# Chunks of the activation parts without padding, at constant places, in a two-block transformer kernel on Trainium2

## The chip, the cores and the metric

The kernel runs on one core of one Trainium2 chip. The metric is device time in microseconds (us) of one execution. Besides the times there is one profiled execution, whose trace gives every instruction's start and duration, engine by engine: PE is TensorE (matrix products), DVE VectorE, ACT ScalarE, POOL GpSimd, and SP the engine that issues nearly all DMAs. The operands of the matrix products lie in SBUF, a memory of 128 partitions; every place below is a byte address within a partition, and it is the same in all of them.

## The reference

Two transformer blocks follow each other on one sequence of 256 tokens with 1,024 features, all in float32.

```python
# first block
xn = rms_norm(x, g); proj = xn @ w_in                 # 1024 -> 3088
y  = concat(moba_attention(q, k, v), gated_linear_attention(...) * silu(gr))
x  = x + y @ w_out
h  = causal_dwconv(rms_norm(x) @ w_ffn_up)            # 1024 -> 2 * 2816
x  = rms_norm(x + (silu(h_gate) * h_val) @ w_ffn_down)
# second block
proj = rms_norm(x) @ w_in_2                           # 1024 -> 6916
ys = short_conv, spatial_gating, stick_breaking, forgetting attention
x  = x + (sum_n sigmoid(gate_n) * (ys_n @ w_branch_n)) @ w_out_2
g, u = split(rms_norm(x) @ w_ffn_in); out = x + (silu(g) * u) @ w_ffn_out
```

Nearly all of the arithmetic is products of 256 tokens with weight matrices that are read once.

## The kernel before

**Split products.** A float32 product is made from three matmuls in the float32r type (`mm3`, lines 184 to 187). Each operand is split into a high and a low part: high times high, low activations times high weights, high activations times low weights. In a matmul one operand is loaded into the array first (the weights, instruction LDWEIGHTS, shown as PEld) and the other streams past it (the moving operand).

**Weights.** The class `Stream` brings the weights in pieces of 128 x 2048 numbers (`raw`, three buffers). ACT copies one half of a piece, 1,024 numbers a partition, to `hi` (line 154) and DVE subtracts to get `lo` (line 155), in five buffers each. A half holds eight weight tiles of 128 numbers, 512 bytes a partition. A buffer of `hi` or `lo` is 4,096 bytes, so every weight tile begins at the same place modulo 512. Call that place 0 from here on: all places below are counted from it, modulo 512.

**Activations.** The moving operands are pairs of tiles (`xh`, `xl`), (`yh`, `yl`) with 8 chunks of 256 tokens (`KD` = 8), and (`hh`, `hl`) with 22 chunks (`KF` = 22). A chunk is 1,024 bytes a partition. In the kernel before the chunks are padded: `new_x` and `new_y` (lines 297 to 301) make tiles of `T + 8` columns and use the first `T`, so that a chunk begins 1,056 bytes behind the one before it, and its place moves by 32. `hh` and `hl` have `T + 4` columns (line 762), 1,040 bytes, and their place moves by 16 with each chunk. By the sizes of the tiles that lie between them, the high parts `xh` and `yh` begin at place 0 and the low parts `xl` and `yl` at 256; `hh` begins at 416 and `hl` at 256.

One pair is not made in these places: the merged branches of the second block, `mh` and `ml` (in `second`, tags `u8a` and `u8b`), have no padding. In the kernel as built all their chunks stand at place 192, before and after the change. Their matmuls are the second block's output projection, 64 weight tiles.

**Which pair feeds what.** In the order of the program, with the number of weight tiles (three matmuls each) whose moving operand the pair is:

- first `xh`, `xl`: normed input, 128 tiles of the first block's projections;
- first `yh`, `yl`: attention outputs, 64 tiles of `w_out`;
- second `xh`, `xl`: 96 tiles, the first six steps of the first feed-forward (`HELD` = 6);
- second `yh`, `yl`: 256 tiles, its other sixteen steps;
- first `hh`, `hl`: 176 tiles of its down projection;
- third `yh`, `yl`: 384 tiles of the second block's projections and gates;
- third `xh`, `xl`: 64 tiles of its branches;
- fourth `yh`, `yl`: 96 tiles of the second feed-forward;
- fourth `xh`, `xl`: its other 256 tiles;
- second `hh`, `hl`: 176 tiles of its down projection.

In `tm` the roles are the other way round: the activations are loaded into the array (half a chunk, 128 tokens) and 256 columns of weights stream, in 336 matmuls in all (lines 185 to 187 with `hi` or `lo` as the moving operand).

**What sets the order.** The program is recorded in the order of the code, and a scheduler orders each engine's instructions. The weights' splitting runs ahead of the matmuls by up to four halves (`AHEAD`). The attention parts are generators that `pump` advances between groups of matmuls. SP issues the loads in the order in which they are recorded: the first weights and `X`, then `late_loads` (lines 91 to 95), then the rest of the weights. `lv` holds masks that the gated linear attention reads on DVE (line 548).

Of the kernel before, what the change touches and what calls it, by code (L numbers as in the profile page):

```python
# [10 lines left out]
F32R = mybir.dt.float32r  # L11
BF = mybir.dt.bfloat16
I32 = mybir.dt.int32
# [5 lines left out]
D, T, FF = 1024, 256, 2816  # L19
KD, KF = D // 128, FF // 128  # L20
# [7 lines left out]
LEVELS = (1, 2, 4, 8, 16, 32)  # L28
# [24 lines left out]
def block_kernel(ctx: ExitStack, tc: tile.TileContext, xT, wst, sm_d, cs_d, lv_d, gup_d, out, dbg=None):  # L53
    nc = tc.nc
# [3 lines left out]
    def pool(name, bufs, **kw):  # L58
        return tc.tile_pool(name=name, bufs=bufs, reuse_waits="tile", **kw)

    const = ctx.enter_context(tc.tile_pool(name="const", bufs=1))
# [6 lines left out]
    def mm_tile():  # L68
        return mmp.tile([128, 512], F32, name="mm", tag="mm")

    def at_tile():
        return atp.tile([128, 512], F32, name="at", tag="at")
# [5 lines left out]
    X = resid.tile([128, KD, T], F32, name="X")  # L78
    sm = const.tile([128, SM_W], F32, name="sm")
    cs = const.tile([128, CS_W], F32, name="cs")  # L80
    lv = const.tile([128, len(LEVELS), 64], I32, name="lv")
    gup = const.tile([17, 256], F32, name="gup")
    nc.scalar.dma_start(out=sm[:, :SM_FIRST], in_=sm_d[:, :SM_FIRST])

# [6 lines left out]
    def late_loads():  # L91
        nc.sync.dma_start(out=cs, in_=cs_d)
        nc.sync.dma_start(out=sm[:, SM_FIRST:], in_=sm_d[:, SM_FIRST:])
        nc.sync.dma_start(out=lv, in_=lv_d)
        nc.sync.dma_start(out=gup, in_=gup_d)

    def par(name):
# [74 lines left out]
    st = Stream()  # L172
    st.load_to(3)
    late_loads()
    identb = const.tile([128, 128], BF, name="identb")
    V.tensor_copy(identb, ident)
# [12 lines left out]
    def fm(ps, xh, xl, ks, start=True, stop=True, steps=0, **kw):  # L189
        ks = list(ks)  # L190
        for n, k in enumerate(ks):
            wh, wl = st.tiles()
            mm3(ps, wh, wl, xh[:, k, :], xl[:, k, :], start and n == 0, stop and n == len(ks) - 1, **kw)
            if n % 4 == 3:
                pump(steps)

    def fm_pair(ps, xh, xl, between=None):

        for n, (a, k) in enumerate([(a, k) for a in range(2) for k in range(KD - 1)] + [(0, KD - 1), (1, KD - 1)]):
            wh, wl = st.tiles()  # L200
            mm3(ps[:, a * T:(a + 1) * T], wh, wl, xh[:, k, :], xl[:, k, :], n == 0, k == KD - 1,
                skip_group_check=True)
            if between and n == KD:
                between()
# [11 lines left out]
    def split_from(h, l, src):  # L216
        S.copy(h, src)
        V.tensor_tensor(l, src, f32(h), op=ALU.subtract)
# [75 lines left out]

    bigs = ctx.enter_context(tc.tile_pool(name="bigs", bufs=1))

    def new_x():
        return tuple(bigs.tile([128, KD, T + 8], F32R, name=n, tag=n)[:, :, :T] for n in ("xh", "xl"))

    def new_y():  # L300
        return tuple(bigs.tile([128, KD, T + 8], F32R, name=n, tag=n)[:, :, :T] for n in ("yh", "yl"))

    nwk = ctx.enter_context(tc.tile_pool(name="nwk", bufs=1))

# [72 lines left out]
    class Boundary:  # L377


        def __init__(self, g, sums=None, first=None, then=None):  # L380
            self.g, self.then = g, then or new_x
            self.h, self.l = (first or new_y)()
            self.ss = SumSq(nwk, "a")
            self.s2, self.g2 = (SumSq(nwk, "b"), sums) if sums is not None else (None, None)
# [18 lines left out]
        def finish(self):  # L403
            if self.s2 is None:
                v, t = (nwk.tile([128, T], F32, name="sq", tag="sq", bufs=3) for _ in range(2))
                self.rb = nwk.tile([128, T], F32, name="rb", tag="rb", bufs=2)
                V.tensor_scalar(v, self.p1, 1.0 / D, EPS, op0=ALU.mult, op1=ALU.add)
                newton(v, self.rb, t, True)
                return
            else:  # L410
                tc.keep_in_program_order(S.preload_act_table_set("natural_log_exp_and_others"))

                v = nwk.tile([128, 4], F32, name="v4")
                V.tensor_scalar(v[:, 0:2], self.p1, 1.0 / D, EPS, op0=ALU.mult, op1=ALU.add)
                V.tensor_scalar(v[:, 2:4], v[:, 0:2], EPS, None, op0=ALU.mult)
                V.scalar_tensor_tensor(v[:, 2:4], self.p2, 1.0 / D, v[:, 2:4], op0=ALU.mult, op1=ALU.add)
                r = inv_sqrt(v, 4, nwk)
                self.r1, r = r[:, 0:2], r[:, 2:4]
            self.r = r
            self.rb = spread(r, nwk)  # L420
# [6 lines left out]


    with pool("first", 1) as wk:
        ss = SumSq(nwk, "a")  # L430
        xh, xl = new_x()
        for k in range(KD):
            scaled(k, par("g_attn"), xh, xl)
# [16 lines left out]
        V.scalar_tensor_tensor(gq, pss[0].rearrange("p (a t) -> p a t", a=2), 0.125, rbb, op0=ALU.mult, op1=ALU.mult)  # L450
        V.tensor_tensor(gk, pss[1].rearrange("p (a t) -> p a t", a=2), rbb, op=ALU.mult)
        yh, yl = new_y()
        cosr = wk.tile([128, T], F32, name="cosr")
        sinr = wk.tile([128, T], F32, name="sinr")
# [281 lines left out]
        if "ya" in dbg:  # L736
            drain(t_gla)
            for k in range(KD):
                t = wk.tile([128, T], F32, name="dbgt")
# [5 lines left out]
        for half in range(2):  # L745
            for d in range(KD):
                a = accs[d // 2]
                fm(a[:, (d % 2) * T:(d % 2 + 1) * T], yh, yl, range(4 * half, 4 * half + 4),
                   start=(half == 0 and d % 2 == 0), stop=(half == 1), steps=2, skip_group_check=True)
                if half and d % 2:  # L750
                    if d == 1:
                        nb_ = Boundary(par("g_ffn"), first=new_x, then=new_y)
                    for e in (d - 1, d):
                        nb_.add(e, a[:, (e % 2) * T:(e % 2 + 1) * T])
            drain(t_gla)
# [3 lines left out]
    def gated_ffn(nb, emit, finish):  # L759

        with pool("ffn", 1) as wk:
            hh, hl = (wk.tile([128, KF, T + 4], F32R, name=n)[:, :, :T] for n in ("hh", "hl"))
            held = []

            def hidden(ps, j):
                split_from(hh[:, j, :], hl[:, j, :], emit(ps, j, wk))

            for j in range(KF):
                ps = mm_tile()
                if j == 0:  # L770
                    fm_pair(ps, nb.h, nb.l, nb.sums)
                    nb.finish()
                    nb.normed()
                else:
                    x = (nb.h, nb.l) if j < HELD else (nb.xh, nb.xl)
                    for half in range(2):
                        fm(ps[:, half * T:(half + 1) * T], *x, range(KD))
                if j < HELD:
                    t = wk.tile([128, 2, T], F32, name="held", tag="held", bufs=3)
                    V.tensor_tensor(t, ps.rearrange("p (a t) -> p a t", a=2),  # L780
                                    nb.rb[:, None, :].to_broadcast([128, 2, T]), op=ALU.mult)
                    hidden(t.rearrange("p a t -> p (a t)"), j)
                else:
                    hidden(ps, j)
            for d in range(KD):
                ps = mm_tile()
                fm(ps[:, :T], hh, hl, range(KF))
                finish(d, ps[:, :T], wk)
# [24 lines left out]
    def first_end(d, ps, wk):  # L813
        if not holder:
            holder.append(Boundary(ggm, par("g_fin")))
        holder[0].add(d, ps)

    gated_ffn(nb_, conv_emit, first_end)
    nb_ = holder[0]

    with pool("second", 1) as wk:
        yh, yl = new_x()
        fr = [wk.tile([128, 2, T], F32, name="fr", tag="t2", bufs=4) for _ in range(2)]
        pss = []
# [11 lines left out]
        xh, xl, rb, r = nb_.h, nb_.l, nb_.rb, nb_.r  # L839
# [22 lines left out]
        pl = at_tile()  # L862
# [31 lines left out]
        for hd in range(2):  # L894
            p, m = 64 - 64 * hd, 96 - 64 * hd
# [214 lines left out]
        if "yb" in dbg:  # L1110
            for k in range(KD):
                t = wk.tile([128, T], F32, name="dbgt")
# [28 lines left out]
    def second_end(d, ps, wk):  # L1141
        V.tensor_tensor(X[:, d, :], X[:, d, :], ps, op=ALU.add)
        nc.sync.dma_start(out=out[:, d, :], in_=X[:, d, :])

    gated_ffn(nb_, swiglu_emit, second_end)
    assert st.used == 16 * N_PIECES, st.used

# [158 lines left out]
```

## Time and profile before

| | |
|---|---|
| median of 3 runs | 751.35 us (750.97 to 751.64) |
| the profiled execution, its own time | 751.71 us |
| span of its trace | 750.0 us |
| PE busy | 736.9 us, 98% of the span |
| DVE, ACT, POOL busy | 71%, 56%, 15% of the span |
| granted TensorE clock, mean | 0.995 of full speed |

The profiled execution is 1.71 us longer than its span, and 0.36 us longer than the median. A matmul's duration in the trace (about 0.28 us) is its passage through the array; several are in it at a time. What counts for the time is the distance from one matmul's start to the next one's start, which the timeline gives to 0.01 us.

### The profile page before, as it was taken

To read this page: it belongs to the slowest core of one execution; us is meant where nothing else is said; L and a number is where in the kernel's file an instruction comes from. 1 tells how busy PE (TensorE), PEld (TensorE's weight loads), DVE (VectorE), ACT (ScalarE), POOL (GpSimd) and SP (SyncE) were. 2 spreads that over 40 slices of the span, in tenths; PEclk is the share of its full clock that TensorE was granted. 3 is DMA by queue.
4 is the path that set the end of the run, shared out by engine and by line. 5 is a ranking of instruction groups with operands and counts; after the bars stand their busy time and mean duration, and the time that the engine had idled before them with its cause. 6 is when DMAs were issued, how large, how long until landed. Compare 5 with 4: busy or idle time off the path is not lost.

```text
span 750.0 us, 14591 instructions
## 1 busy us (share of the span) xinstructions
PE 736.9 (98%) x6042; PEld 718.9 (96%) x6042; DVE 535.8 (71%) x805; ACT 423.2 (56%) x689; POOL 113.9 (15%) x125
## 2 busy tenths in 40 slices
PE   8997999999999999999999999999999999999998
PEld 7996889999999999999998999999999999999998
DVE  6679756899998776556785787766889855555441
ACT  7574666577767655545457476444467644444330
POOL 3067100214222111221000001100223100000000
PEclk9998999999999999999999999999999999999999
DMA  8742332364555554544443444554446555455530
GB/s 304 291 146 86 113 113 83 143 225 149 189 209 185 189 205 169 176 163 169 169 169 113 169 147 141 198 190 170 169 170 225 177 204 183 173 195 197 188 127 22
DMA packets 19813, 127.51 MB, mean 170 GB/s; under 512 B 2322, under 2 KB 3747, under 8 KB 5027
## 3 DMA queue, kind: packets, MB, share of 16 engines
q1 hardware_dynamic: 19602, 126.56, 47.7%
q8 instruction: 47, 0.77, 0.4%
q14 instruction: 20, 0.16, 0.1%
q10 hardware_dynamic: 144, 0.02, 0.0%
HBM read 125.52 MB, written 1.05 MB: 169 GB/s over the span
## 4 chain that ended last, share of the span: by engine, by line
PE 90%; DVE 6%; ACT 1%; DMA 1%; issue 1%; SPq 0%; DVEq 0%; ACTq 0%
PE mm L185 28%; PE mm L186 28%; PE mm L187 28%; DVE lo L155 2%; DMA X<-in_x 1%; PE at L698 1%; PE at L371 1%; DVE Qb L533 1%; DVE AT L548 1%; PE at L363 1%; DVE xl L283 0%; PE at L927 0%; PE at L372 0%; DVE cv L803 0%; PE at L942 0%
## 5 line engine op out<-in xcount | busy, mean ns | idle before, releaser
L155 DVE TENSOR_TENSOR lo<-raw,hi 128x1024 fp32r<-128x1024 f32 (+1 forms) x236 | 296.2, 1259 | 137.0 <-ACT hi L154 136.1
L154 ACT CAST hi<-raw 128x1024 fp32r<-128x1024 f32 (+1 forms) x236 | 244.5, 1041 | 216.7 <-PE mm L186 170.1
L185 PE MATMUL mm<-yh,hi 128*128 128x256 f32 x800 | 225.0, 283 | 0.8 <-DVE cv L803 0.8
L186 PE MATMUL mm<-yl,hi 128*128 128x256 f32 x800 | 224.0, 281 | 0.0
L187 PE MATMUL mm<-yh,lo 128*128 128x256 f32 x800 | 223.9, 281 | 0.0
L185 PE MATMUL mm<-xh,hi 128*128 128x256 f32 x544 | 153.8, 284 | 1.5 <-ACT hi L154 1.3
L187 PE MATMUL mm<-xh,lo 128*128 128x256 f32 x544 | 153.8, 285 | 1.1 <-DVE lo L155 1.0
L186 PE MATMUL mm<-xl,hi 128*128 128x256 f32 x544 | 152.6, 282 | 0.1
L185 PEld LDWEIGHTS mm<-yh,hi 128*128 128x128 f32 x800 | 150.1, 188 | 1.6 <-ACT hi L154 0.9
L186 PEld LDWEIGHTS mm<-yl,hi 128*128 128x128 f32 x800 | 150.8, 189 | 0.7 <-issue 0.6
L187 PEld LDWEIGHTS mm<-yh,lo 128*128 128x128 f32 x800 | 150.7, 188 | 0.1
L185 PEld LDWEIGHTS mm<-xh,hi 128*128 128x128 f32 x544 | 102.5, 189 | 2.9 <-ACT hi L154 2.1
L187 PEld LDWEIGHTS mm<-xh,lo 128*128 128x128 f32 x544 | 102.5, 189 | 2.8 <-DVE lo L155 2.1
L186 PEld LDWEIGHTS mm<-xl,hi 128*128 128x128 f32 x544 | 102.7, 189 | 0.7 <-DVE xl L283 0.5
L186 PE MATMUL mm<-hl,hi 128*128 128x256 f32 x352 | 99.0, 281 | 0.0
L187 PE MATMUL mm<-hh,lo 128*128 128x256 f32 x352 | 98.8, 281 | 0.0
L185 PE MATMUL mm<-hh,hi 128*128 128x256 f32 x352 | 98.5, 281 | 0.0
L186 PEld LDWEIGHTS mm<-hl,hi 128*128 128x128 f32 x352 | 66.4, 189 | 0.0
L187 PEld LDWEIGHTS mm<-hh,lo 128*128 128x128 f32 x352 | 66.3, 188 | 0.0
L185 PEld LDWEIGHTS mm<-hh,hi 128*128 128x128 f32 x352 | 66.1, 188 | 0.0
L277 POOL TENSOR_TENSOR ssa<-ssa,sq 128x256 f32<-128x256 f32 x20 | 18.7, 936 | 120.9 <-ACT sq L276 120.4
L806 POOL TENSOR_TENSOR cv<-cv 128x256 f32<-128x256 f32 x22 | 23.5, 1067 | 81.0 <-DVE cv L803 76.0
(333 smaller groups left out, 961.3 us busy)
## 6 DMA issues: line engine op xcount, KB each, us to landing
raw<-in_w SPq DMA_DIRECT2D x115, 1024.0 KB, 4.8
raw<-in_w SPq DMA_DIRECT2D x3, 512.0 KB, 8.3
out<-X SPq DMA_DIRECT2D x8, 128.0 KB, 1.9
sm<-in_sm SPq DMA_DIRECT2D x1, 814.5 KB, 13.4
X<-in_x SPq DMA_DIRECT2D x3, 256.0 KB, 7.3
cs<-in_cs SPq DMA_DIRECT2D x1, 706.0 KB, 11.3
raw<-in_w SPq DMA_DIRECT2D x2, 256.0 KB, 4.1
X<-in_x SPq DMA_DIRECT2D x2, 128.0 KB, 3.4
```

The costliest lines, as they stand in the source:

```text
L154: a = S.copy(hi[:, c:c + step], raw[:, c:c + step])
L155: b = V.tensor_tensor(lo[:, c:c + step], raw[:, c:c + step], f32(hi[:, c:c + step]), op=ALU.subtract)
L185: PE.matmul(ps, lh, rh, start=start, stop=False, **kw)
L186: PE.matmul(ps, lh, rl, start=False, stop=False, **kw)
L187: PE.matmul(ps, ll, rh, start=False, stop=stop, **kw)
L277: (V if self.n >= 6 else G).tensor_tensor(self.s, self.s, q, op=ALU.add)
L363: PE.transpose(pts[hd][:, j * 128:(j + 1) * 128], Ps[hd][:, j * 128:(j + 1) * 128], ident)
L371: PE.matmul(o, vs_[hd][0], PTs[hd][:, 0:256], start=True, stop=False, skip_group_check=True)
L533: V.tensor_tensor(q.rearrange("p x (n h) -> p x n h", h=h), qv[rows, :, :, 1, :], ev[rows, :, :, 1, :], op=ALU.mult)
L548: V.copy_predicated(o, lv[:, n, None, :].to_broadcast([128, 8, 64]).rearrange("p e (n h) -> p e n h", h=h), pm.rearrange("p (e n h) -> p e ...
L698: PE.matmul(ps[:, c:c + n], qb[:, a, hd, i * 128:(i + 1) * 128], kT[:, a, :n], start=True, stop=False, skip_group_check=True)
L806: G.tensor_tensor(c[0], c[0], c[1], op=ALU.mult)
```

## The change

`bigs` and the feed-forward pools no longer hold padded tiles. A new function `placed` makes a tile of `n * T + 128` columns and cuts out of it `n` chunks of `T` columns without padding, from column `first` on. All chunks of a part then stand at one place modulo 512. A list, `places`, names the first column for each pair in the order in which the pairs are made; both parts of a pair have the same one.

`X` and the new tiles of 8,704 bytes are multiples of 512, so `xh`, `xl`, `yh` and `yl` all begin at place 0, and a first column of 48 puts their chunks at place 192. `hh` and `hl` (23,040 bytes) both begin at 416, and column 72 puts them at 192. So the places are, in the order of the list above: 192, 208, 176, 192, 192, 192, 192, 160, 448 and 448. In `tm`, where the activations are loaded, the streaming weights stand at 320 against them throughout; before, that distance moved with the chunk.

To make room, `lv` leaves the pool `const` for the pool `first`, whose space later stages use again, and its load is recorded behind that of `gup`. Everything behind it in SBUF moves by 1,536 bytes, three times 512.

```diff
-    lv = const.tile([128, len(LEVELS), 64], I32, name="lv")
...
-        nc.sync.dma_start(out=lv, in_=lv_d)
         nc.sync.dma_start(out=gup, in_=gup_d)
...
+    places = {"x": [(48, 48), (44, 44), (48, 48), (112, 112)], "y": [(52, 52), (48, 48), (48, 48), (40, 40)],
+              "h": [(72, 72), (8, 8)]}
+
+    def placed(pl, name, n, first):
+
+        t = pl.tile([128, n * T + 128], F32R, name=name, tag=name)
+        return t[:, first:first + n * T].rearrange("p (k t) -> p k t", t=T)
+
+    def new_pair(c):
+        return tuple(placed(bigs, c + p, KD, o) for p, o in zip("hl", places[c].pop(0)))
+
     def new_x():
-        return tuple(bigs.tile([128, KD, T + 8], F32R, name=n, tag=n)[:, :, :T] for n in ("xh", "xl"))
+        return new_pair("x")
 
     def new_y():
-        return tuple(bigs.tile([128, KD, T + 8], F32R, name=n, tag=n)[:, :, :T] for n in ("yh", "yl"))
+        return new_pair("y")
...
     with pool("first", 1) as wk:
+        lv = wk.tile([128, len(LEVELS), 64], I32, name="lv")
+        nc.sync.dma_start(out=lv, in_=lv_d)
...
-            hh, hl = (wk.tile([128, KF, T + 4], F32R, name=n)[:, :, :T] for n in ("hh", "hl"))
+            hh, hl = (placed(wk, "h" + p, KF, o) for p, o in zip("hl", places["h"].pop(0)))
```

On PE, DVE and ACT the instructions stand in the same order before and after; only their addresses differ. On SP, early in the program, two loads change places. Before:

```order
L92 DMA cs<-in_cs 128x1412
L93 DMA sm<-in_sm 128x1629
L94 DMA lv<-in_lv 128x384
L95 DMA gup<-in_gup 17x256
L141 DMA raw<-in_w 128x2048 x109
```

After the change, at the same place of SP's order:

```order
L91 DMA cs<-in_cs 128x1412
L92 DMA sm<-in_sm 128x1629
L93 DMA gup<-in_gup 17x256
L441 DMA lv<-in_lv 128x384
L139 DMA raw<-in_w 128x2048 x109
```

The masks `lv` are now loaded behind the small table `gup`; the weights behind both keep their place.

## Rows read from the trace of the kernel before

**Rows 1.** The page: the span, each engine's busy time, the granted clock by slices.

```profile
span 750.0 us, 14591 instructions
PE 736.9 (98%) x6042; PEld 718.9 (96%) x6042; DVE 535.8 (71%) x805; ACT 423.2 (56%) x689; POOL 113.9 (15%) x125
...
PEclk9998999999999999999999999999999999999999
```

**Rows 2.** The page's chain of work that ended last, by engine.

```profile
PE 90%; DVE 6%; ACT 1%; DMA 1%; issue 1%; SPq 0%; DVEq 0%; ACTq 0%
```

**Rows 3.** PE's waits: line, waited for, us in total, times, longest us.

```profile
PE at L542 <- DVE Qb L533: 4.5, 2, 3.1
PE mm L185 <- ACT hi L154: 1.3, 1, 1.3
PE at L117 <- DVE ones L111: 1.1, 1, 1.1
PE mm L187 <- DVE lo L155: 1.0, 1, 1.0
PE mm L185 <- DVE cv L803: 0.8, 1, 0.8
PE at L698 <- DVE AT L548: 0.6, 1, 0.6
```

**Rows 4.** Timeline: start us, duration us, engine, line; a matmul and the weight loads.

```profile
708.70 0.28 PE L185 MATMUL mm<-hh,hi 128*128 128x256 f32 x1
708.70 0.19 PEld L186 LDWEIGHTS mm<-hl,hi 128*128 128x128 f32 x1
708.82 0.28 PE L186 MATMUL mm<-hl,hi 128*128 128x256 f32 x1
708.83 0.19 PEld L187 LDWEIGHTS mm<-hh,lo 128*128 128x128 f32 x1
...
709.07 0.28 PE L185 MATMUL mm<-hh,hi 128*128 128x256 f32 x1
```

**Rows 5.** Timeline, PE: chunk nine of the same output, and chunk ten's start.

```profile
710.49 0.28 PE L185 MATMUL mm<-hh,hi 128*128 128x256 f32 x1
...
710.83 0.28 PE L185 MATMUL mm<-hh,hi 128*128 128x256 f32 x1
```

**Rows 6.** Timeline, PE: first matmul of the output projection, and of what follows.

```profile
535.86 0.28 PE L185 MATMUL mm<-mh,hi 128*128 128x256 f32 x1
...
558.47 0.28 PE L185 MATMUL mm<-yh,hi 128*128 128x256 f32 x1
```

**Rows 7.** Timeline, PE: second feed-forward, fourth x pair's first, hh's first and last matmul.

```profile
592.93 0.28 PE L185 MATMUL mm<-xh,hi 128*128 128x256 f32 x1
...
683.81 0.28 PE L185 MATMUL mm<-hh,hi 128*128 128x256 f32 x1
...
746.29 0.28 PE L187 MATMUL mm<-hh,lo 128*128 128x256 f32 x1
```

**Rows 8.** Timeline, PE: first feed-forward, matmul behind a wait, hh's first, the next stage.

```profile
203.75 0.28 PE L186 MATMUL mm<-yl,hi 128*128 128x256 f32 x1
...
271.78 0.28 PE L185 MATMUL mm<-hh,hi 128*128 128x256 f32 x1
...
334.39 0.28 PE L185 MATMUL mm<-yh,hi 128*128 128x256 f32 x1
```

**Rows 9.** Timeline, PE: the first block's output projection, first matmul, and of what follows.

```profile
121.65 0.28 PE L185 MATMUL mm<-yh,hi 128*128 128x256 f32 x1
...
144.28 0.28 PE L185 MATMUL mm<-xh,hi 128*128 128x256 f32 x1
```

**Rows 10.** Timeline, PE: chunk six of the fourth x pair, and chunk seven's start.

```profile
595.07 0.28 PE L185 MATMUL mm<-xh,hi 128*128 128x256 f32 x1
...
595.42 0.28 PE L185 MATMUL mm<-xh,hi 128*128 128x256 f32 x1
```

**Rows 11.** The tile lv: its DMA and its reads, and its time to landing.

```profile
L548 DVE COPY_PREDICATED AT<-lv,at x6: 686/718/1321, 58.9 to 83.0; 128x512 f32<-128x512 int32 x6
L94 SPq DMA_DIRECT2D lv<-in_lv x1: 328/328/328, 10.0 to 10.0; - x1
...
DMA to landing us min/median/max: 12.6/12.6/12.6
```

## The prediction

> **What bounds the kernel now.** I read the page's busy times first. PE is busy for 98% of the span, and the granted clock reads nine tenths or more of the upper level, 2.4 GHz, in 39 of 40 slices [rows 1], so nothing is to be had there. The chain of waits says the same: 90% of what set the end is PE, 6% DVE [rows 2]. The waits that ended idle times of PE sum to 9.3 us, nearly all of them in the start and in the first block's attention [rows 3]. What is left is how far apart the matmuls start. The timeline shows that in single rows. In a piece of the second down projection the load of the next weights starts in the hundredth of a microsecond in which a matmul starts (708.70 and 708.70, 708.82 and 708.83), it lasts 0.19 us, and the next matmul starts 0.12 us after the one before [rows 4]. So the stream is a chain of weight loads, each beside the streaming of the matmul ahead of it.
>
> That distance is not the same everywhere, although the instructions are. The three matmuls of chunk four of `hh` (places 480 and 320) take 709.07 - 708.70 = 0.37 us [rows 4], those of chunk nine (places 48 and 400) 710.83 - 710.49 = 0.34 us [rows 5], 123 and 113 ns a matmul. Both lie in one output of one projection, with the same shapes and the same engines at work, and no wait is marked at either. The only thing that differs by design is where the moving chunks lie against the weights. That is what the change alters, so the sum is made in ns per matmul, stage by stage.
>
> **What a matmul costs in each stage now.** I take stretches in which nothing but these matmuls runs, from the first start to the start of the next stage, and divide by their number, so that the rounding to 0.01 us does not count:
>
> - fourth `xh`, `xl`: 683.81 - 592.93 = 90.88 us for 256 x 3 = 768 matmuls, 118.33 ns [rows 7];
> - second `yh`, `yl` in the first feed-forward: 271.78 - 203.75 = 68.03 us for 575 matmuls (the 192 tiles left, less one matmul), 118.31 ns [rows 8]; the padding is the same, and I use 118.33 for all pairs of eight chunks with it;
> - `hh`, `hl`: 334.39 - 271.78 = 62.61 us for 528, 118.58 ns in the first feed-forward [rows 8], 746.29 - 683.81 = 62.48 us for 527 starts, 118.56 ns in the second [rows 7];
> - the first block's output projection goes through half the chunks at a time: 144.28 - 121.65 = 22.63 us for 192, 117.86 ns [rows 9];
> - `mh`, `ml`, without padding, both parts at place 192: 558.47 - 535.86 = 22.61 us for 192, 117.76 ns [rows 6].
>
> The last one is the layout that the change gives to the others. It is the only constant place in the trace, and so it carries the sum.
>
> **The change part by part.** Place 192, unpadded, five pairs. Four of them have eight chunks: the first x pair (384 matmuls), the second y pair (768), the third y pair (1,152) and the third x pair (192), 2,496 in all; the fifth is the first `hh`, `hl` (528). They go from 118.33 and 118.58 to 117.76: 2,496 x 0.57 ns = 1.42 us and 528 x 0.82 ns = 0.43 us, together 1.85 us off. These matmuls are the path itself; no other work lies over them. A little of it is given back: in the first block PE waits 4.5 us for DVE's operands [rows 3], and PE that comes earlier waits longer there. What it can lose is at most what was gained ahead of it, 384 x 0.57 = 0.22 us for the whole stage, and I leave it in.
>
> Other constant places. The first y pair stands at 208 (192 matmuls), the second x pair at 176 (288), the fourth y pair at 160 (288), the fourth x pair at 448 (768) and the second `hh`, `hl` at 448 (528): 2,064 matmuls, for which no row shows a constant place. A chunk's own rows do not settle it. Place 192 itself reads 595.42 - 595.07 = 0.35 us for three matmuls in the padded x pair, where the low part is at 448 [rows 10], and 0.353 in `mh`. So a chunk's triple depends on its neighbours as well. The ends are single chunks: 113 ns [rows 5] and 123 ns [rows 4], 4.5 below and 5.6 above 117.76. Over 2,064 matmuls that is 9.3 us less or 11.6 us more, but a whole stage has never stood near either end, because in the walk a dear chunk and a cheap one alternate, and the six stretches above lie within 0.8 ns. I take the row of `mh` again, the nearest in kind: 192 x 0.10 = 0.02, 288 x 0.57 = 0.16 twice, 768 x 0.57 = 0.44 and 528 x 0.80 = 0.42, together 1.20 us off. For the range I allow 1.8 ns below (the 0.35 us chunk and its rounding, 116 ns a matmul) and 2.2 above (120 ns, between `mh` and the dear chunk): 3.7 us less or 4.5 us more.
>
> `tm`. Here 336 matmuls get a constant distance of 320 where they had a changing one. No row shows it; at 2 ns either way it is 0.7 us, and I take nothing.
>
> `lv`. Its load goes behind that of `gup`. It was issued at 10.0 and landed 12.6 us later, at about 22.6; its first reader starts at 58.9 [rows 11]. The cover of 36 us hides a swap of two neighbours, and a delay of more than that would be needed to cost anything. All loads of weights stay behind the same set of transfers. The writes of the chunks by ACT and DVE move to other addresses too; those engines are not what PE waits for, beyond [rows 3], so they cost nothing.
>
> **The sum.** 1.85 + 1.20 = 3.05 us off. The profiled execution has 750.0 us of span [rows 1] and 751.71 us as its own time, so it would become 748.66. It lies 0.36 us above the median of the runs, 751.35; taken off the median the sum gives 748.3 us, 0.41% less.
>
> **A rule weighed against the trace.** The distance changes with the chunk's place by up to 10 ns [rows 4, 5]. The Trainium skill says otherwise: in "TensorE: Matmul & The Clock Gate", section "Step-by-step: what each phase is for", the array reads the moving operand and the weights through two ports of their own, so that loading the next weights takes nothing from the running matmul; and "SBUF — State Buffer", section "SBUF: two separate sides", adds that PE waits for no one. By that rule the place of a chunk would be worth nothing and the time would stay at 751.35. The trace disagrees in the size of 9% between two chunks, but agrees to half a percent in the means over a stage, which is all the change can use.
>
> **The rivals.**
>
> - *The place matters for single chunks, not for a mean* (no change). The two operands sweep past each other in each matmul whatever the distance, what a chunk loses its neighbour gets back, and the 0.57 ns of `mh` is its own stage's. For it: all stretches lie between 117.76 and 118.58. Against it: the unpadded stretch is the lowest of all. Time: 751.3, or down to 749.9 if half of the sum arrives.
> - *Constant places settle lower than `mh`* (faster by more). If all 5,088 moved matmuls came to the 0.35 us chunk, 116.7 ns, against 118.36 in the mean, that is 8.5 us off: 742.9. For it: that chunk holds the high parts at 192 and the low parts at 448, both places of the change [rows 10]. Against it: `mh` stands at 192 throughout and does not reach it.
> - *Place 448 is a dear one* (slower). The padding spreads dear and cheap places over a stage; a constant place repeats one of them in each matmul. At the dear chunk's 123.3 ns the 1,296 matmuls of the second feed-forward at 448 would lose 1,296 x 4.9 = 6.3 us, against 2.2 us won elsewhere: 755.5. It decides from 118.43 + 2.2 / 1.296 = 120.1 ns on. For it: no row shows a constant 448. Against it: the padded x pair passes 448 in its 0.35 us chunk, one of its cheapest.
> - *The change does not reach the moving operands.* The built kernel has its chunks at the places named, so I give it nothing.
>
> **How the numbers follow.** The forecast, constant places near the row of `mh`, gets 0.62; its own range is 747.0 to 749.8. Lower places get 0.13, no change 0.17, slower 0.08. The range for 8 in 10 takes the 3.7 us below, 744.6, and above it the no-change case, up to 751.4; what is left out is the slower rival and the end of the faster one. A measurement of this kernel can tell about 0.2%, 1.5 us, from no change. Faster by more than that (under 749.85) has most of the forecast and all of the lower case: 0.73. Within it: 0.20. Slower: 0.07.
>
> **What would show it.** In the profile after, the same stretches: the second feed-forward's x pair and `hh` at 117.8 ns a matmul, the first `hh` at 117.8, and `mh` unchanged at 117.76. Within a stage the triples of all chunks should be alike, 0.35 us, where they went from 0.34 to 0.37. It is wrong if a stage at 192 differs from `mh` by more than 0.3 ns (then the distance modulo 512 is not what decides), if 448 is a stage of its own above 119 or below 117, or if the waits of PE grow by what the matmuls save.

## The result, and the profile after

The changed kernel takes 740.34 us in the median of four runs, against 751.37 for the kernel before: a ratio of 0.9854 (95% interval 0.9805 to 0.9904). The single times lie far apart, 737.61, 737.96, 742.71 and 743.25 us, where those of the kernel before agree within 0.7. The forecast was 748.3, with a range that ended at 744.6. It was wrong, on the side of its second rival. Every ratio in this document leaves out executions more than 1.5% above the fastest of their kernel; of the kernels below, that is one execution, at 743.26 us with all pairs at place 192.

The page of the profiled execution (742.71 us, one of the two longer ones), span and busy times:

```profile
span 741.0 us, 14591 instructions
PE 726.3 (98%) x6042; PEld 708.6 (96%) x6042; DVE 536.1 (72%) x805; ACT 423.0 (57%) x689; POOL 114.8 (15%) x125
```

The instructions are the same in number, PE is as dense as before, and it is done 9.0 us earlier. The timeline of the kernel after, PE alone (start us, duration us, line, what), gives the first matmul of each stage, and two pieces of the first feed-forward:

```profile
120.14 0.28 PE L183 MATMUL mm<-yh,hi 128*128 128x256 f32 x1
...
143.02 0.28 PE L183 MATMUL mm<-xh,hi 128*128 128x256 f32 x1
...
178.84 0.28 PE L183 MATMUL mm<-yh,hi 128*128 128x256 f32 x1
...
200.50 0.28 PE L185 MATMUL mm<-yh,lo 128*128 128x256 f32 x1
202.28 0.36 PE L183 MATMUL mm<-yh,hi 128*128 128x256 f32 x1 [1.50 <-DVE cv L815]
202.47 0.28 PE L184 MATMUL mm<-yl,hi 128*128 128x256 f32 x1
...
270.20 0.28 PE L183 MATMUL mm<-hh,hi 128*128 128x256 f32 x1
...
332.38 0.28 PE L183 MATMUL mm<-yh,hi 128*128 128x256 f32 x1
...
528.11 0.28 PE L183 MATMUL mm<-mh,hi 128*128 128x256 f32 x1
...
549.87 0.28 PE L183 MATMUL mm<-yh,hi 128*128 128x256 f32 x1
...
584.78 0.28 PE L183 MATMUL mm<-xh,hi 128*128 128x256 f32 x1
...
675.23 0.28 PE L183 MATMUL mm<-hh,hi 128*128 128x256 f32 x1
...
737.30 0.28 PE L185 MATMUL mm<-hh,lo 128*128 128x256 f32 x1
```

From these and [rows 6 to 9], stage by stage; the distance is the stage's time through its number of matmuls, where nothing else runs in it:

| stage (place after) | before, us | after, us | ns a matmul, before and after |
|---|---|---|---|
| to the end of the first projections (192) | 121.65 | 120.14 | |
| first block's output projection (208) | 22.63 | 22.88 | 117.86, 119.17 |
| first feed-forward, up (176, 192) | 127.50 | 127.18 | its last 575: 118.31, 117.79 |
| first down projection (192) | 62.61 | 62.18 | 118.58, 117.77 |
| second block up to its merge (192) | 201.47 | 195.73 | |
| `mh`, `ml` (192, as before) | 22.61 | 21.76 | 117.76, 113.33 |
| second feed-forward, first six steps (160) | 34.46 | 34.91 | |
| its other steps (448) | 90.88 | 90.45 | 118.33, 117.77 |
| its down projection and the end (448) | 66.19 | 65.77 | 118.56, 117.78 |

The differences sum to 9.0 us. Four stretches did what was forecast: the last 575 matmuls of the first feed-forward, its down projection, and the two at place 448 are at 117.8. Most of the gain that was not forecast is in the second block: 5.74 us, where 1,344 matmuls by 0.57 ns were to give 0.77. With it `mh`, whose places were not changed, went from 117.76 to 113.33, another 0.85 us. The first projections gained 1.51 us where 0.22 were forecast. And the first feed-forward shows both in one stage: the 191 distances from 178.84 to 200.50 take 21.66 us, 113.4 ns each; then PE waits, and the next 575, with the same tiles at the same places, take 270.20 - 202.47 = 67.73 us, 117.8 each.

So one place has two distances. The weight loads of `mh` differ with them. Those of its products high times high, in the kernel before (duration min/median/max in ns, first and last start):

```profile
L185 PEld LDWEIGHTS mm<-mh,hi x64: 187/192/192, 535.7 to 558.0; 128*128 128x128 f32 x64
```

and in the kernel after:

```profile
L183 PEld LDWEIGHTS mm<-mh,hi x64: 187/188/188, 528.0 to 549.4; 128*128 128x128 f32 x64
```

At 117.8 some weight loads take 192 ns; at 113.3 none does.

PE's longest wait in total in the kernel after answers to [rows 3]:

```profile
PE at L554 <- DVE Qb L545: 5.9, 4, 3.2
```

Before, it was 4.5 us. The wait for `cv` went from 0.8 to 1.5 us (the row at 202.28 above). In these two, 2.1 us of what the matmuls saved went into waits.

### The profile page after: what moved, and what is told of

Same layout as the page of the kernel before. It is cut to its first block, busy times and chain, and to the rows that moved or that the text cites. A ratio compares the mean times of both kernels' runs of the same rounds, so it can differ in the third digit from the quotient of the medians.

```text
span 741.0 us, 14591 instructions
## 1 busy us (share of the span) xinstructions
PE 726.3 (98%) x6042; PEld 708.6 (96%) x6042; DVE 536.1 (72%) x805; ACT 423.0 (57%) x689; POOL 114.8 (15%) x125
## 4 chain that ended last, share of the span: by engine, by line
PE 89%; DVE 7%; issue 2%; ACT 1%; DMA 1%; SPq 0%; DVEq 0%; ACTq 0%
PE mm L184 27%; PE mm L183 27%; PE mm L185 27%; DVE lo L153 2%; PE at L381 1%; DMA X<-in_x 1%; DVE Qb L545 1%; DVE AT L560 1%; PE at L373 1%; PE at L710 1%; DVE xl L281 1%; DVE Dl L539 0%; PE at L939 0%; DVE cv L814 0%; ACT hi L152 0%
## 5 line engine op out<-in xcount | busy, mean ns | idle before, releaser
L275 POOL TENSOR_TENSOR ssa<-ssa,sq 128x256 f32<-128x256 f32 x20 | 18.6, 930 | 118.8 <-ACT sq L274 118.3
```

Source lines behind the costliest of these rows:

```text
L275: (V if self.n >= 6 else G).tensor_tensor(self.s, self.s, q, op=ALU.add)
```

## The experiments

Theory A: at a constant place a stream of matmuls settles into one of a few steady distances; at 192 there are two, and what restarts the stream decides which. Theory B: the place alone decides, perhaps by more than its rest modulo 512. Rival C: the move of everything by 1,536 bytes won the time.

### The changed kernel once more

No edit.

> The changed kernel once more, to see a second trace of it. Theory A (two states): at place 192 a stream of matmuls has two steady distances, 113.3 and 117.8 ns, and whatever interrupts the stream (a wait, other matmuls) decides which one follows; the place alone does not. Then this trace has the same addresses but other stages in the low state: the stretch of the first feed-forward from 202 us to its end, 1,100 matmuls at 117.8 in the first trace, is at 113.3 in some executions, which is worth 4.9 us, and single times lie near 738 or near 743. Theory B (the place decides, modulo more than 512 bytes): every stage has the distance that it had in the first trace, within 0.1 ns, and the time is again 742 to 743.

Measured: 731.30 and 743.08 us. The profile is of the execution at 731.30; its timeline, PE:

```profile
202.52 0.28 PE L184 MATMUL mm<-yl,hi 128*128 128x256 f32 x1
...
267.71 0.28 PE L183 MATMUL mm<-hh,hi 128*128 128x256 f32 x1
...
327.55 0.28 PE L183 MATMUL mm<-yh,hi 128*128 128x256 f32 x1
...
544.86 0.28 PE L183 MATMUL mm<-yh,hi 128*128 128x256 f32 x1
...
579.12 0.28 PE L183 MATMUL mm<-xh,hi 128*128 128x256 f32 x1
...
666.17 0.28 PE L183 MATMUL mm<-hh,hi 128*128 128x256 f32 x1
```

The 575 matmuls behind the same wait take 65.19 us, 113.4 ns, and the down projection 59.84 for 528, 113.3. The 768 at place 448 take 87.05 us, 113.3. In the first trace all three stood at 117.8. It is the same program with the same addresses, so theory B falls, and 448 has both distances too. Place 160 also has two: the stage from 544.86 to 579.12 takes 34.26 us, where it took 34.91, and most of its matmuls stand 117.0 to 117.6 ns apart in the mean of twelve, where they stood at 120.0. The sizes fit the single times: 575 + 528 matmuls by 4.4 ns are 4.9 us (743 to 738), the 1,296 at 448 another 5.8 and the stage at 160 another 0.65 (to 731.7).

### All pairs at place 192

```diff
-    places = {"x": [(48, 48), (44, 44), (48, 48), (112, 112)], "y": [(52, 52), (48, 48), (48, 48), (40, 40)],
-              "h": [(72, 72), (8, 8)]}
+    places = {"x": [(48, 48)] * 4, "y": [(48, 48)] * 4, "h": [(72, 72)] * 2}
```

> All ten pairs at place 192; the 208, 176, 160 and both 448 places are gone. Theory A: the stages that stood at 119.2, 119.2 and 120.0 ns (768 matmuls) fall to 113.3 or 117.8, which is 1.2 to 4.8 us, and the 1,296 matmuls of the second feed-forward that stood at 117.8 stay or fall to 113.3, 0 to 5.8 us: 731 to 741 us, with single times in steps of some us. Theory B: each stage takes a distance of its own, the same in all executions, and times agree within 1 us.

Measured: 736.08 us, ratio 0.9764 (0.9711 to 0.9818); single times 730.22, 735.04, 737.11 and 743.26. In the profiled execution (735.04) the first feed-forward's down projection is at 117.8 (62.19 us for 528) and the second feed-forward at 113.3 (87.03 us for 768). As theory A says. The spread is 13 us, with a granted clock of 0.995 to 0.998 in all four, and the intervals of this kernel and of the changed one overlap.

The second block shows the restarts one by one. The third y pair is interrupted by other matmuls, most of them of the attention parts. Two of its streams, one soon behind the other, in the first trace of the changed kernel; timeline, PE:

```profile
413.83 0.28 PE L184 MATMUL mm<-yl,hi 128*128 128x256 f32 x1
...
417.57 0.28 PE L184 MATMUL mm<-yl,hi 128*128 128x256 f32 x1
...
419.40 0.28 PE L185 MATMUL mm<-yh,lo 128*128 128x256 f32 x1
...
425.06 0.28 PE L185 MATMUL mm<-yh,lo 128*128 128x256 f32 x1
```

The first takes 3.74 us for 33 matmuls, 113.3 ns, the second 5.66 us for 48, 117.9. Between them stand other matmuls and a short stream of nine, and no wait of PE. Twelve such streams there are longer than 24 matmuls. In every trace with this pair at 192 (both of the changed kernel, this one, and the last two below, in the last with the low part at 448) the same seven end at 113.3 and the same five at 117.8, whether the stage before them stood at 113.3, 117.8 or 120.0. The twelfth is at 113.3 and, in the changed kernel, runs on without a break through the third x pair and `mh`. The stretches that differ between the two traces of the changed kernel begin elsewhere: behind PE's wait at 202 us, and behind the norm's sums in the second feed-forward.

### The masks' move alone

```diff
-    lv = const.tile([128, len(LEVELS), 64], I32, name="lv")
...
-        nc.sync.dma_start(out=lv, in_=lv_d)
...
     with pool("first", 1) as wk:
+        lv = wk.tile([128, len(LEVELS), 64], I32, name="lv")
+        nc.sync.dma_start(out=lv, in_=lv_d)
```

> The kernel before with one part of the change: lv goes to the other pool and its load behind gup, so that everything behind it moves by 1,536 bytes; the padding stays. Theory A: 751.4 us as before (750.9 to 751.9), the padded stages at 118.3 and 118.6 ns. Rival C (the shift of all addresses is what won): 740 to 746 us, and the unpadded mh, ml at 113.3 ns.

Measured: 751.26 us, ratio 0.9997 (0.9987 to 1.0006). The same weight loads of `mh`:

```profile
L183 PEld LDWEIGHTS mm<-mh,hi x64: 187/192/192, 535.3 to 557.6; 128*128 128x128 f32 x64
```

Rival C falls: moved by 1,536 bytes and entered from padded stages, `mh` is as it was before, with loads of 192 ns. The move costs nothing, either. The larger tiles of the change (8,704 instead of 8,448 bytes, four of them) are not in this run, and what lies behind them stands elsewhere in the changed kernel; that its own addresses do not decide is shown by its repeat above.

### All pairs at place 0

```diff
+    places = {"x": [(0, 0)] * 4, "y": [(0, 0)] * 4, "h": [(24, 24)] * 2}
```

> Padding away, and all ten pairs at place 0, the weights' own place modulo 512. If being constant is what counts, as theory A says in its simple form, stages have steady distances from the same two values and the time is 731 to 745 us. If the place counts as well (theory A with the place, theory B), place 0 has other steady distances: from the padded stages' spread of 113 to 123 ns a chunk anything from 730 to 775 us, and all stages alike.

Measured: 757.67 us, ratio 1.0084 (1.0069 to 1.0099); the four single times within 0.12 us. Timeline, PE:

```profile
272.95 0.28 PE L183 MATMUL mm<-hh,hi 128*128 128x256 f32 x1
...
336.31 0.28 PE L183 MATMUL mm<-yh,hi 128*128 128x256 f32 x1
...
596.80 0.28 PE L183 MATMUL mm<-xh,hi 128*128 128x256 f32 x1
...
688.96 0.28 PE L183 MATMUL mm<-hh,hi 128*128 128x256 f32 x1
```

63.36 us for 528 and 92.16 us for 768 are 120.0 ns in both. The weight loads of `hh`, high times high:

```profile
L183 PEld LDWEIGHTS mm<-hh,hi x352: 192/192/192, 272.8 to 751.8; 128*128 128x128 f32 x176
```

And `mh`, still at 192, from its first matmul to the next stage's:

```profile
540.05 0.29 PE L183 MATMUL mm<-mh,hi 128*128 128x256 f32 x1
...
561.83 0.28 PE L183 MATMUL mm<-yh,hi 128*128 128x256 f32 x1
```

Without padding at place 0 the kernel is 0.8% slower than with it. Being constant is not what won; it is the place. Place 0 shows one distance in these stages, 120.0, with each weight load of `hh` at 192 ns. `mh` takes 21.78 us, 113.4 ns, although the stage ahead of it is at 120.0.

### Thirty places in three kernels

A different place for each pair, for instance

```diff
+    places = {"x": [(4, 4), (12, 12), (28, 28), (36, 36)],
+              "y": [(8, 8), (16, 16), (24, 24), (32, 32)],
+              "h": [(44, 44), (80, 80)]}
```

> One look at ten places, a different one for each pair, in the order of the program: 16, 32, 48, 64, 80, 96, 112, 128, 144 and 224. Theory A with the place: every place has its own small set of steady distances, as 0 has 120.0 alone and 192 and 448 have 113.3 and 117.8; a place whose only one is 113.3 would end the dependence on the state. Rival: distances come from three values alone (113.3, 117.8, 120.0) and the stage, not the place, picks one: then the stages show them in the order in which they stood before, 115, 119, 119, 117, 118, 114, 113, 120, 118, 118 ns. The sum of the stages gives 735 to 765 us.

> As the first look, at 240, 256, 272, 288, 304, 320, 336, 352, 368 and 384. Theory A with the place: distances by place, between 113.3 and 123; if a shift of 256 changes nothing (as 192 and 448 suggest), 256 has 120.0 alone, as 0 has, and 240 to 384 repeat what the first look shows at 16 to 128. Rival (the stage decides): the same order of distances over the stages as in the first look.

> As the first look, at 400, 416, 432, 464, 480, 496 and, in steps of 8 around the two places of the change, 184, 200, 440 and 456. Theory A with the place: 416 like 160 (119 to 120), 432 like 176 (119.2), 464 like 208 (119.2), and if the two-state region is narrow, 184, 200, 440 and 456 are already out of it. Rival (the stage decides): the same order of distances over the stages as in the first look.

Measured, one execution each: 751.99, 745.51 and 752.32 us. The last stage with eight chunks, 768 matmuls, stands at 144 in the first kernel, 368 in the second, 440 in the third; timelines, PE:

```profile
593.05 0.28 PE L183 MATMUL mm<-xh,hi 128*128 128x256 f32 x1
...
684.20 0.28 PE L183 MATMUL mm<-hh,hi 128*128 128x256 f32 x1
```

```profile
590.50 0.28 PE L183 MATMUL mm<-xh,hi 128*128 128x256 f32 x1
...
677.57 0.28 PE L183 MATMUL mm<-hh,hi 128*128 128x256 f32 x1
```

```profile
591.53 0.28 PE L183 MATMUL mm<-xh,hi 128*128 128x256 f32 x1
...
683.67 0.28 PE L183 MATMUL mm<-hh,hi 128*128 128x256 f32 x1
```

That is 118.7, 113.4 and 120.0 ns. The commonest mean distance of twelve neighbouring matmuls at each place, with the place 256 bytes on behind the stroke (from the three traces; 0, 192 and 448 from the runs above, 176 and 208 from the changed kernel's first trace, 160 from both of its traces). At 144, 176, 208 and 224 and their partners the blocks of one stage differ by up to about 1 ns in turn, and a value between them stands:

| place | ns | place | ns |
|---|---|---|---|
| 0 / 256 | 120.0 / 120.0 | 128 / 384 | 118.8 / 118.8 |
| 16 / 272 | 116.7 and 118.8 / 118.8 | 144 / 400 | 118.6 / 119.1 |
| 32 / 288 | 116.7 / 116.7 | 160 / 416 | 120.0 and about 117.4 / 119.0 |
| 48 / 304 | 118.3 / 118.3 | 176 / 432 | 119.2 / 119.2 |
| 64 / 320 | 117.8 / 117.8 and, for 47 matmuls, 113.3 | 184 / 440 | 120.0 / 120.0 |
| 80 / 336 | 120.0 / 120.0 | 192 / 448 | 113.3 and 117.8, both |
| 96 / 352 | 120.0 / 120.0 | 200 / 456 | 120.0 / 120.0 |
| 112 / 368 | 113.3 / 113.3 | 208 / 464 | 119.2 / 119.1 |
| | | 224 / 480 | 118.3 / 118.3 |
| | | 240 / 496 | 117.2 / 117.2 |

The rival falls: the same stage shows 118.7, 113.4 and 120.0 by its place. Most places agree with the one 256 on. Eight bytes beside 192 and 448 the low distance is gone. And 112 shows it alone where 192 shows two. Most places were seen in one stage of one execution, so a second distance is not excluded there.

### All pairs at 112, and all at 368

```diff
+    places = {"x": [(28, 28), (28, 28), (28, 28), (28, 28)],
+              "y": [(28, 28), (28, 28), (28, 28), (28, 28)],
+              "h": [(52, 52), (52, 52)]}
```

and with 92 and 116 in place of 28 and 52.

> All ten pairs at place 112, which in the first look stood at 113.3 ns in all blocks but the first. Theory A with the place: 112 has 113.3 as its only steady distance, whatever restarts the stream; then the 5,088 matmuls that stood at 118.4 gain 5 ns each, 25 us, and the time is 725 to 729 us with single times within 1 us of each other. Rival (112 has two states as 192 has, and the look met the low one): 727 to 745 us with single times some us apart.

> All ten pairs at place 368, which is 112 + 256. If places repeat every 256 bytes, as the looks suggest (0 and 256, 32 and 288, 80 and 336, 112 and 368 agree within 0.1 ns): the same time as at 112, 725 to 729 us, single times within 1 us. If they do not: stages at other distances, and a time apart from that of 112 by more than 1.5 us.

Measured: 730.92 us, ratio 0.9724 (0.9711 to 0.9738), and 731.11 us, ratio 0.9731 (0.9718 to 0.9744). The single times lie between 729.58 and 732.14 and between 730.35 and 732.47. In the median both beat the changed kernel, whose fastest execution, 731.30, is as short; they don't differ from each other. Timeline of the kernel at 112, PE:

```profile
202.44 0.35 PE L183 MATMUL mm<-yh,hi 128*128 128x256 f32 x1 [1.85 <-DVE cv L816]
...
269.45 0.28 PE L183 MATMUL mm<-hh,hi 128*128 128x256 f32 x1
...
329.29 0.28 PE L183 MATMUL mm<-yh,hi 128*128 128x256 f32 x1
...
579.96 0.28 PE L183 MATMUL mm<-xh,hi 128*128 128x256 f32 x1
...
667.00 0.28 PE L183 MATMUL mm<-hh,hi 128*128 128x256 f32 x1
```

59.84 us for 528 and 87.04 us for 768: 113.3 ns in both, behind a wait of PE and behind other matmuls alike. The spread of 13 us at 192 is down to 2.6. That is theory A with the place, though not in its clean form: right behind other matmuls some blocks of twelve stand near 118.8 ns. They do not stay there. The stream in the third y pair that stood at 117.9 to its end at place 192 reads here:

```profile
416.40 0.28 PE L185 MATMUL mm<-yh,lo 128*128 128x256 f32 x1
...
417.47 0.28 PE L185 MATMUL mm<-yh,lo 128*128 128x256 f32 x1
...
421.89 0.28 PE L185 MATMUL mm<-yh,lo 128*128 128x256 f32 x1
```

Nine matmuls at 118.9 ns, then 39 at 113.3. All twelve streams there end at 113.3, at 112 and at 368. So a restart decides at 192, and at 112 its effect is gone within some ten to twenty matmuls.

The time missed its expectation by 2 us or more. PE's waits sum to 11.8 us in the profiled execution, 2.5 more than before. In `tm` the streaming weights now stand at 400 against the loaded activations. The starts of those 336 matmuls, without gaps over 0.15 us, are 119.8 ns apart in the mean, where they were 118.3 in the kernel before and, at 320, 115.7 in the changed one: some 0.5 us lost against the kernel before, 1.4 against the changed one. And in the profiled execution PE's clock falls behind its wait at the first feed-forward's seventh step. Busy times in two stretches (us; busy and count of PE, PEld, DVE, ACT, POOL; granted clock; DMA share, GB/s):

```profile
200.30:202.40 2.10, 0.28 (x3) 0.09 (x1) 2.10 (x6) 1.71 (x4) 0.00 (x0) 1.00 0.79 332
202.60:206.00 3.40, 3.40 (x18) 3.40 (x18) 3.40 (x7) 2.57 (x5) 1.06 (x2) 0.52 0.20 31
```

After 2.1 us in which PE had almost nothing to do, the granted clock reads 0.52, so nearly all of that stretch is at 1.2 GHz: 18 matmuls in 3.4 us, where at 113.3 ns there would be 30. That is 1.4 us. But the profiled execution is the longest of the five, 732.14 us. Those at 729.58 and 730.92 have a mean granted clock of 1.000, which 3.4 us at 0.52 would lower by 0.002; the fall of the clock does not explain why the median lies above 729. The rest of the miss is not taken apart.

### A small matmul ahead of each step

All pairs at place 192, as above, and:

```diff
+            def kick():
+                PE.matmul(at_tile()[:, :128], identb, causalb, start=True, stop=True)
+
             for j in range(KF):
                 ps = mm_tile()
+                if j:
+                    kick()
...
             for d in range(KD):
                 ps = mm_tile()
+                kick()
                 fm(ps[:, :T], hh, hl, range(KF))
```

> All ten pairs at place 192, and one more small matmul (128 columns in bf16, its result is not read) before each step of both feed-forwards but the first and before each output of their down projections, 58 in all at 0.1 to 0.2 us, 6 to 12 us of added work. Theory A says that a restart decides the state: each step of 48 or 66 matmuls then has a state of its own, the long stretches of 768 and 528 matmuls in one state are gone, and the same restart gives the same state each time, so single times lie within 2 us of each other (730 to 750 us), where they spread over 13 us without the restarts. Rival (the state belongs to the execution, not to the restart): stages keep one state throughout, and the spread stays near 13 us.

Measured: 737.75 us, ratio 0.9817 (0.9803 to 0.983); the four single times within 0.53 us, at place 192, where without these matmuls they spread over 13. Timeline, PE:

```profile
284.38 0.23 PE L782 MATMUL at<-causalb,identb 128*128 128x128 bf16 x1
284.42 0.36 PE L183 MATMUL mm<-hh,hi 128*128 128x256 f32 x1
284.62 0.28 PE L184 MATMUL mm<-hl,hi 128*128 128x256 f32 x1
...
292.01 0.23 PE L782 MATMUL at<-causalb,identb 128*128 128x128 bf16 x1
292.05 0.36 PE L183 MATMUL mm<-hh,hi 128*128 128x256 f32 x1
292.25 0.28 PE L184 MATMUL mm<-hl,hi 128*128 128x256 f32 x1
```

Each restart reads the same (0.04 us, then 0.20), and behind it the stream is at 113.3 each time: in the first down projection 32 of 40 blocks of twelve are, and the other eight, at 122.4, hold the first matmuls behind a restart; the mean of all forty is 115.2. So the restart decides, the same one in the same way, as theory A says, and as the twelve streams of the second block say without any added matmul. The wait of PE for DVE is no such restart: behind it the stream is at 117.8 in the first trace of the changed kernel and at 113.3 in its repeat. That this is because the wait ends at another moment each time is argued, not shown.

### Parts 256 bytes apart

```diff
+    places = {"x": [(28, 92), (92, 28), (28, 92), (28, 92)],
+              "y": [(0, 64), (28, 92), (48, 112), (8, 72)],
+              "h": [(24, 88), (44, 108)]}
```

> One look at pairs whose high and low parts stand 256 bytes apart, each chunk without padding, in the order of the program: high and low at 112/368, 0/256, 368/112, 112/368, 0/256, 192/448, 112/368, 32/288, 112/368 and 80/336. If only the place modulo 256 counts, each pair has the distance of its place with both parts alike: 113.3, 120.0, 113.3, 113.3, 120.0, 113.3 or 117.8, 113.3, 116.7, 113.3 and 120.0 ns, within 0.1. Rival (the period is 512, and equal distances 256 apart are two separate places that happen to agree): the pairs take other values, as the padded walk did, where high at 192 beside low at 448 stood at 116 ns.

Measured, one execution: 739.78 us. The stage at 112 and 368, 768 matmuls; timeline, PE:

```profile
584.05 0.28 PE L183 MATMUL mm<-xh,hi 128*128 128x256 f32 x1
...
671.14 0.28 PE L183 MATMUL mm<-hh,hi 128*128 128x256 f32 x1
```

113.4 ns; the others read 120.0 (0/256, 80/336), 116.7 (32/288), 113.3 (112/368 and 368/112, but for five of sixteen blocks at 119.5 in the third x pair, each the first twelve matmuls behind a change from 192/448), and 113.3 with 117.8 (192/448). In these pairs the place modulo 256 decides which distances there are. The high and low parts of the padded x and y pairs, 256 bytes apart, were therefore always at one place, and only the walk by 32 bytes a chunk moved it.

## Why the prediction was wrong

- **What bounds the kernel** held: the distance of the matmuls' starts, and the place of the chunk in it. The runs at 0 and at 112 differ in places alone and lie 27 us apart. That it is a chain of weight loads is not shown: the load at 708.83 starts before the one at 708.70 has ended [rows 4], so they overlap. The loads are longer where the distance is longer; no run tells which causes which.
- **"It is the only constant place in the trace, and so it carries the sum"** is the step that failed. The row of `mh` [rows 6] was read as the distance of place 192. It is one of two. Entered from padded stages it was at 117.8, in the kernel before and in the run with the masks' move alone; in the trace after and in the repeat, entered from a stage at 113.3, it was at 113.3. Entered from a stage at 120.0, with the other pairs at place 0, it was at 113.4, so what counts is not the distance of the stage ahead. In all traces without padding it is at the low one; what the padded stage ahead does to it stays open. The term that was mis-sized: 2,496 + 528 matmuls at 192 by 0.57 and 0.82 ns were to give 1.85 us; the second block, with 1,152 + 192 of them, gave 5.74 us alone.
- **The other constant places** were taken at the same value. 448 did read 117.8 in the first trace (0.43 + 0.42 us, forecast 0.44 + 0.42), and 113.3 in the repeat. 208 and 160 cost time, 0.25 and 0.45 us, where 0.02 and 0.16 us of gain were forecast; 208 and 176 stand at 119.2, 160 at 120.0 in the first trace and 117.4 in the repeat. The median, 740.34 us, lies between executions whose long stretches fell into one distance or the other, near 738 and near 743.
- **The rival that came nearest**, "constant places settle lower", had 0.13. Its ground, the 0.35 us chunk [rows 10], pointed the right way; what spoke against it, that `mh` stands at 192 and does not reach it, was a reading of one stretch, behind padded stages alone. The steady low distance is 113.3, below that chunk's 116.
- **The slower rival** was sound, but not at 448: place 0 does repeat a dear distance in each matmul, 120.0, and the kernel at 0 is slower than with padding.
- **The range** took 1.8 ns below `mh` for the unknown places, and nothing at all for place 192 itself, since that one counted as known.
- **`lv` at nothing** held: 751.26 against 751.45 us. **`tm` at nothing** was 0.9 us too little: 336 matmuls went from 118.3 to 115.7 ns in the mean. **The wait in the first block** was to take back at most 0.22 us, the gain forecast ahead of it; behind a larger gain it grew by 1.4, from 4.5 to 5.9 us.
- **What was to show it wrong** showed it: a stage at 192 differs from 117.76 by 4.4 ns. What the prediction would have read from it, that the distance modulo 512 is not what decides, does not follow: the place sets which distances there are, and the restart picks one of them.

Still open is what the two states at 192 are inside the engine. The runs show that a restart picks one, that the weight loads at 117.8 and 120.0 are partly or all 192 ns long, not 188, and which places showed which distance. They also show that 112 comes back to the low one behind a restart and 192 need not; not why.

## What to carry to other kernels

Where matmuls follow each other without a gap, measure the distance of their starts by stage, not PE's busy share: it read 98% at 758, 751, 741 and 732 us alike, and the distance differed by up to 6% with the place of the moving operand. Make that place the same for all chunks, but try several: the wrong constant is worse than a padded walk. And read one stretch as one sample: a steady value may have a second one beside it. A repeat of the same profile may not show it, since `mh` read 117.8 in both padded traces; the same tiles behind another stage, or behind a restart, showed it.

## What the hardware showed

- The distance of 256-column float32r matmuls with a weight load each depends on the moving operand's address modulo 256 bytes, with the weights at one place: 113.3 ns at 112, 120.0 at 0, 80 and 96. In `tm`, where the weights stream, moving the loaded activations from 192 to 112 raised it from 115.7 to 119.8 in the mean. No run moved the weights, so it is not shown that the distance between the two addresses is what counts. The Trainium skill ("TensorE: Matmul & The Clock Gate", section "Step-by-step: what each phase is for") says that loading the next weights takes no read bandwidth from the running matmul. These runs show that the two are not independent: with nothing changed but the place of the moving operand, each weight load of `hh` takes 192 ns at place 0 instead of 188 at 112, and each matmul 6.7 ns more. Whether read bandwidth is what is lost they do not show.
- Places 192 and 448 have two steady distances, 113.3 and 117.8 ns, and a stream stayed in one of them for up to 152 us (at 448, from 584.78 to 737.30 us in the first trace after). Within a stream at one of these places no change from one to the other was seen without other matmuls or a wait between.
- At 192 the same interruption by other matmuls left the stream at the same distance in twelve of twelve cases, in five traces; at 112 and 368 all twelve came back to 113.3.
- A faster PE met the same wait for DVE earlier: 0.8 us before [rows 3], 1.85 us at place 112, and behind it, in the profiled execution, 3.4 us at a granted clock of 0.52.
